# Nine modulation vectors per layer: three move one FFN stage later, and three of the first stage change from VectorE alone to VectorE, GpSimd and ScalarE

## The chip, the core and the metric

The kernel runs on one core of a Trainium2 chip. The core has a matrix engine (TensorE, PE in the rows), an elementwise engine (VectorE, DVE), an activation engine (ScalarE, ACT), a programmable engine (GpSimd, POOL) and an engine that here only issues transfers (SyncE, SP). Each works through its own instructions in order. The metric is device time in microseconds (us), the median of the runs; less is better.

## What is computed

Two layers of a diffusion backbone over 256 latent and 256 context tokens of width 1024. Each layer is FFN, token mixer, FFN; every one of these has a shift, a scale and a gate, which are slices of one modulation product per layer and stream. Cut to what matters here:

```python
act_l = jax.nn.silu(c)
act_c = jax.nn.silu(c_ctx)
for i in range(DEPTH):
    mod_l = (act_l @ w_mod[i] + b_mod[i])[:, None, :]          # 9 vectors of 1024
    mod_c = (act_c @ w_mod[i][:, :n_c] + b_mod[i][:n_c])       # 9 in layer 0, 5 in layer 1
    ...
def ffn_sublayer(x, mods, base, g_pre, g_post, w_in, w_out):
    h = modulated_norm(x, g_pre, mods[base], mods[base + 1])
    return x + 0.5 * mods[base + 2] * rms_norm(swiglu(h, w_in, w_out), g_post)
```

Vectors 0 to 2 belong to the first FFN of a layer, 3 to 5 to its mixer, 6 to 8 to its second FFN.

## The kernel before

**Matrix work.** Every weight is brought as chunks of 128x1024 f32. SyncE loads a chunk into a ring of four buffers ("raw"); ScalarE rounds it into `wh` (L220), VectorE makes the rest `wl` = raw - wh (L221), and TensorE does three products for each pair (L227, L228, L229; 24 matmuls of 512 columns for a chunk, called a unit below). `wh` and `wl` have three buffers each. TensorE's order is written out by hand and is the same in both kernels; the other engines' orders come from a scheduler that follows the program's emission order and a few marks (`after`).

**The modulation vectors.** One vector is eight tiles of 128x1024 of `w_mod`. A tile is multiplied by the activation (a broadcast row `act`) and summed along its row, once for the context stream and once for the latent stream (layer 1's vectors 5 to 8 need the latent stream alone). `mod_flow` knows two ways for a tile with two streams:

- "both on VectorE" (`both`, layer 0 with j >= JB): two VectorE instructions `jk` (L329), each with its sum.
- "split": one `jk` on VectorE for the latent stream, then GpSimd multiplies the tile in place by the context row (L333), then ScalarE sums it (L306). The tile's buffer is free only after that sum.

A tile with one stream is one `jk`.

**Where the tiles go.** They are spread over the units of three FFN stages; `stepper` is called once a unit and hands out tiles at a rate (a sum of costs over a total) after a number of skipped units. Stage A is the first FFN of layer 0 (about 60 to 460 us): its tiles share the raw ring with the weights and are loaded by SyncE, and beside them GpSimd computes the set-up of a state space (S5) (L205 to L210 on tiles `s5...`), whose tables SyncE writes out with eight transfers (`s5d<-s5tab`); a hyena filter is computed too. Stage B is the second FFN of layer 0 (about 1212 to 1560 us), stage C the first FFN of layer 1 (about 1595 to 1945 us). In B and C a tile has a ring of its own with two buffers (`mraw`), and its load is issued by GpSimd (L298), in order between GpSimd's other work. B and C also make the S5 tables of layer 1 (`s5_tables`, one slice per eight units in B and per five in C), which go back and forth between GpSimd (`bb`, `vvt`, L1191 to L1213), VectorE (`rin`, `wt`, L205 to L210, L1222 to L1224), ScalarE (`rin`), TensorE (`pn`, L1230, L1240) and transfers.

Per unit of its second part, a stage thus has on VectorE: `wl`, the gate (L547, L548, and `gg`, L234, per two units), the `jk`s, and in B and C the table work.

Of the kernel before, what the change touches and what calls it, by code (L numbers as in the profile page):

```python
# [79 lines left out]
RAW0 = 16  # L80
WPF = 2
OW = 1.0
JB = 5


def layout(i):
# [77 lines left out]
def build(tc, A):  # L164
# [10 lines left out]
    def dma(o, i):  # L175
        return nc.sync.dma_start(o, i)

    def after(*ins):

        stack = ExitStack()  # L180
        for i in ins:
            stack.enter_context(tc.issue_after(i.ins))
        return stack

    with st, tc.manual_schedule(engines={mybir.EngineType.PE}):
# [71 lines left out]
        def mod_steps(l, js, act, raw=None):  # L257
            if callable(act):
                act = act()
            for j in js:  # L260
                ss = [1] if l == 1 and j >= 5 else [0, 1]
                for k in range(KT):
                    w = raw() if raw else rp.tile([P, D], F32, tag="raw", name="raw")
                    dma(w, A["wmod"][l, j, k])
                    c = j * KT + k
                    both = l == 0 and j >= JB
                    for s in ss if both else [1]:
# [17 lines left out]
        def mod_flow(l, js, act, raw=None):  # L285

            if callable(act):
                act = act()  # L290
            tiles = [(j, k) for j in js for k in range(KT)]
            ws, back = {}, []

            def load(n):
                if n < len(tiles):
                    j, k = tiles[n]
                    ws[n] = raw() if raw else rp.tile([P, D], F32, tag="raw", name="raw")
                    (G.dma_start if raw else dma)(ws[n], A["wmod"][l, j, k])  # L298

            def finish():  # L300
                while back:
                    back.pop(0)()

            def sums(w, s, c):
                with after(mark["wh"]):
                    S.activation(w, w, AF.Copy, scale=0.5, accum_out=md[l][:, s, c : c + 1])  # L306

            def bias(j, ss):
                for s in ss:
                    m = md[l][:, s, j * KT : (j + 1) * KT]  # L310
                    V.tensor_tensor(m, m, bmt[l][:, j * KT : (j + 1) * KT], op=ALU.add)

            if raw:
                load(0)
                yield
            for n, (j, k) in enumerate(tiles):
                finish()
                if not raw:
                    load(n)
                c = j * KT + k  # L320
                w = ws.pop(n)
                ss = [1] if l == 1 and j >= 5 else [0, 1]
                both = l == 0 and j >= JB
                fast = ss if both else [1]
                slow = [s for s in ss if s not in fast]
                for s in fast:
                    jk = sp.tile([P, D], BF16, tag="sq", name="jk", bufs=1)
                    with after(mark["wl"]):
                        V.scalar_tensor_tensor(  # L329
                            jk, w, 0.5, act[s], op0=ALU.mult, op1=ALU.mult, accum_out=md[l][:, s, c : c + 1]  # L330
                        )
                for s in slow:
                    G.tensor_tensor(w, w, act[s], op=ALU.mult)  # L333
                    back.append(lambda w=w, s=s, c=c: sums(w, s, c))
                if k == KT - 1:
                    back.append(lambda j=j, ss=ss: bias(j, ss))
                if raw:
                    load(n + 1)
                yield
            finish()  # L340
# [6 lines left out]
        def pre_coeff(l, base, gi, streams):  # L347
            a = cp.tile([P, 2, KT], F32, tag="pa", name="pa", bufs=2)
            for s in streams:
                V.scalar_tensor_tensor(  # L350
                    a[:, s], md[l][:, s, (base + 1) * KT : (base + 2) * KT], 1.0, ngt[l][:, gi], op0=ALU.add, op1=ALU.mult
                )
                V.tensor_scalar(a[:, s], a[:, s], RMS_D, None, op0=ALU.mult)
            return lambda s, k: (a[:, s, k : k + 1], md[l][:, s, base * KT + k : base * KT + k + 1])

        def gate_rows(l, base, gi, fac, streams):
            gr = cp.tile([P, 2, D], F32, tag="grow", name="grow", bufs=1)
            gc = cp.tile([P, 2, KT], F32, tag="gc", name="gc", bufs=2)
            for s in streams:
                V.scalar_tensor_tensor(  # L360
                    gc[:, s], md[l][:, s, (base + 2) * KT : (base + 3) * KT], fac * RMS_D, ngt[l][:, gi], op0=ALU.mult, op1=ALU.mult
                )
            s0, n = streams[0], len(streams)
            ps = psy.tile([P, 512], F32, tag="py", name="psg")
            T.transpose(ps[: n * KT, :P], gc[:, s0:].rearrange("p s k -> p (s k)"), ident)
            gs = sp.tile([P, 512], F32, tag="t", name="gs")[:, :P]
            S.activation(gs[: n * KT], ps[: n * KT, :P], AF.Copy)
            gd = dp.tile([1, 2 * D], F32, tag="gd", name="gd", bufs=2)
            dma(gd[:, : n * D].rearrange("o (k p) -> (o k) p", p=P), gs[: n * KT])
            dma(gr[:, s0:].rearrange("p s d -> p (s d)"), gd[:, : n * D].to_broadcast([P, n * D]))  # L370
            return gr
# [229 lines left out]
        def act_load():  # L601
            a = [xp.tile([P, D], F32, tag="xr", name="act") for _ in range(2)]
            for s in range(2):
                dma(a[s], actd[s].to_broadcast([P, D]))
            return a
# [29 lines left out]
        def stepper(gens, total, skip=0):  # L635

            todo = [g for g, _ in gens]
            rate = sum(c for _, c in gens) / total
            state = {"credit": 0.0, "skip": skip}

            def step(weight):
                if state["skip"]:
                    state["skip"] -= 1
                    return
                state["credit"] += rate * weight
                while todo and state["credit"] > 1e-6:
                    try:
                        next(todo[0])
                        state["credit"] -= 1.0
                    except StopIteration:  # L650
                        todo.pop(0)

            return step
# [15 lines left out]
        with ExitStack() as fs:  # L669
# [127 lines left out]
                        acts.extend(act_load())  # L797
                return acts

            st0 = stepper([(mod_flow(0, [2, 3, 4], acts0), 25), (mod_flow(0, [5, 6, 7, 8], acts0), 33)], 46, 12)  # L800

            half = [0]

# [11 lines left out]
        for l in range(L):  # L815
            last = l == L - 1
            toks = TLAT if last else TALL
            streams = [1] if last else [0, 1]

            nx = dict(src=xd, out=None, keep=toks)  # L820
            late = mixer(E, l, h, late, toks, streams, nx)
            h = nx["h"]

            with ExitStack() as fs:
                gp = Gates(fs, f"B{l}")
                if last:
                    n3 = dict(src=xd, out=A["out"], keep=[])
                    ffn(l, 1, h, late, toks, n3, gp, lambda w: None, lambda: gate_rows(l, 6, 5, 0.5, streams), lambda: None)
                else:
                    n3 = dict(src=xd, out=None, keep=TALL)  # L830

                    def fill1():
                        n3.update(coeff=pre_coeff(1, 0, 0, [0, 1]), h=new_h())

                    x1, raw1 = mod_ring(fs, "mrB")
                    st1 = stepper([(mod_flow(1, [0, 1, 2, 3, 4], act_load, raw1), 42)], 50, 4)
                    tg1 = ahead(fs, gp, "s5p", range(0, 3))

                    def step1(w):
                        st1(w)  # L840
                        tg1()

                    late = ffn(l, 1, h, late, toks, n3, gp, step1, lambda: gate_rows(l, 6, 5, 0.5, streams), fill1, xpool2=x1)
                    h = n3["h"]
            if not last:
                with ExitStack() as fs:
                    gp = Gates(fs, "C")
                    n4 = dict(src=xd, out=None, keep=TLAT)

                    def fill2():  # L850
                        n4.update(coeff=pre_coeff(1, 3, 2, [0, 1]), h=new_h())

                    x2, raw2 = mod_ring(fs, "mrC")
                    st2 = stepper([(mod_flow(1, [5, 6, 7, 8], act_load, raw2), 34)], 50, 4)
                    tg2 = ahead(fs, gp, "s5q", range(3, 8))

                    def step2(w):
                        st2(w)
                        tg2()

                    late = ffn(1, 0, h, late, TALL, n4, gp, step2, lambda: gate_rows(1, 0, 1, 0.5, [0, 1]), fill2, xpool2=x2)
                    h = n4["h"]
# [1395 lines left out]
```

## Time and profile before

| what | value |
|---|---|
| median of 3 runs | 2597.41 us (2596.99 to 2599.07) |
| the profiled execution | 2597.24 us |
| its span in the trace | 2595.4 us |
| TensorE busy | 2482.5 us, 96% |
| VectorE busy | 1750.1 us, 67% |
| ScalarE busy | 1079.3 us, 42% |
| GpSimd busy | 671.6 us, 26% |

The span is the time from the first to the last instruction of the profiled execution. Busy shares are means over stages that differ much: VectorE has 67% over the span, and far more in parts of A, B and C.

### The profile page before, as it was taken

What the parts mean: (1) busy time and instruction counts of PE and PEld (TensorE: products, weight loads), DVE (VectorE), ACT (ScalarE), POOL (GpSimd) and SP (SyncE); (2) the same over time, 40 slices, a digit from 0 to 9 for tenths busy, and PEclk for the clock granted to TensorE, in tenths of its full rate; (3) what the DMA queues carried; (4) which work ended last, traced back from release to release, by engine and by line L of the source; (5) the groups of instructions that cost most, each with busy time, mean ns of one, the idle gap of its engine ahead of it and who ended that gap; (6) DMA issues with size and microseconds to landing.
All of it is one profiled execution on the core that took longest, in us unless ns stands there. A gap on an engine that the chain in (4) does not pass through costs nothing. (4 is left out here: it accounts for less than half of the span.)

```text
span 2595.4 us, 38077 instructions
## 1 busy us (share of the span) xinstructions
PE 2482.5 (96%) x14606; PEld 2096.0 (81%) x14606; DVE 1750.1 (67%) x2624; ACT 1079.3 (42%) x1828; POOL 671.6 (26%) x692
## 2 busy tenths in 40 slices
PE   6988999999999898999999999999999999998998
PEld 3866888887778776888778888888889889997996
DVE  6888995455645798557998637885435667776664
ACT  5345323454543223434444424332234555355443
POOL 4894000100101784003665403540001012000000
PEclk8999999999999999999999999999999999999999
DMA  6336675223232232343565544676542335865564
GB/s 244 107 118 229 233 256 194 78 82 82 75 109 86 76 97 86 105 159 135 190 213 203 196 162 148 223 239 189 173 138 78 94 111 179 324 227 197 179 192 133
DMA packets 138819, 411.07 MB, mean 158 GB/s; under 512 B 27096, under 2 KB 45321, under 8 KB 135821
## 3 DMA queue, kind: packets, MB, share of 16 engines
q1 hardware_dynamic: 124812, 353.61, 41.8%
q0 software_dynamic: 12672, 45.59, 5.2%
q10 hardware_dynamic: 1152, 9.44, 0.9%
q8 instruction: 115, 1.88, 0.3%
q14 instruction: 68, 0.55, 0.1%
HBM read 374.41 MB, written 34.16 MB: 157 GB/s over the span
## 5 line engine op out<-in xcount | busy, mean ns | idle before, releaser
L221 DVE TENSOR_TENSOR wl<-raw,wh 128x1024 fp32r<-128x1024 f32 x424 | 557.1, 1314 | 468.2 <-ACT wh L220 461.4
L220 ACT ACTIVATE wh<-raw 128x1024 fp32r<-128x1024 f32 x424 | 448.9, 1059 | 748.0 <-issue 184.8
L229 PE MATMUL pin<-hh,wl 128*128 128x512 f32 (+1 forms) x1468 | 529.9, 361 | 18.7 <-DVE wl L221 18.6
L227 PE MATMUL pin<-hh,wh 128*128 128x512 f32 (+1 forms) x1468 | 531.6, 362 | 11.8 <-DVE hh L415 7.8
L228 PE MATMUL pin<-hl,wh 128*128 128x512 f32 (+1 forms) x1468 | 528.7, 360 | 1.7 <-DVE hl L418 1.6
L229 PEld LDWEIGHTS pin<-hh,wl 128*128 128x128 f32 x1468 | 282.5, 192 | 64.7 <-DVE wl L221 24.9
L227 PEld LDWEIGHTS pin<-hh,wh 128*128 128x128 f32 x1468 | 282.8, 193 | 56.9 <-DVE hh L415 9.4
L228 PEld LDWEIGHTS pin<-hl,wh 128*128 128x128 f32 x1468 | 282.6, 193 | 42.7 <-DVE hl L418 3.1
L246 POOL TENSOR_TENSOR r<-v,mhalf 128x1 f32<-128x1 f32 (+2 forms) x46 | 31.4, 682 | 1030.4 <-DVE v L245 931.8
L1345 PE MATMUL pm<-hh,wh 128*128 128x512 f32 (+1 forms) x704 | 251.5, 357 | 0.0
L1347 PE MATMUL pm<-hh,wl 128*128 128x512 f32 (+1 forms) x704 | 245.2, 348 | 0.2 <-DVE wl L221 0.2
L1346 PE MATMUL pm<-hl,wh 128*128 128x512 f32 (+1 forms) x704 | 245.0, 348 | 0.0
L461 PE MATMUL y<-wh,gg 128*128 128x512 f32 x448 | 177.2, 396 | 0.0
L463 PE MATMUL y<-wh,gg 128*128 128x512 f32 x448 | 177.2, 396 | 0.0
L462 PE MATMUL y<-wl,gg 128*128 128x512 f32 x448 | 177.2, 396 | 0.0
L1345 PEld LDWEIGHTS pm<-hh,wh 128*128 128x128 f32 x704 | 134.1, 190 | 18.1 <-issue 2.5
L1347 PEld LDWEIGHTS pm<-hh,wl 128*128 128x128 f32 x704 | 133.8, 190 | 17.8 <-DVE wl L221 0.4
L1346 PEld LDWEIGHTS pm<-hl,wh 128*128 128x128 f32 x704 | 134.1, 191 | 15.0
L329 DVE SCALAR_TENSOR_TENSOR jk<-raw,act 128x1024 bf16<-128x1024 f32 x88 | 117.6, 1336 | 5.0 <-DMA raw<-wmod 4.1
L333 POOL TENSOR_TENSOR mraw<-mraw,act 128x1024 f32<-128x1024 f32 x40 | 102.6, 2565 | 49.6 <-DVE jk L329 48.3
L227 PE MATMUL pm<-hh,wh 128*128 128x256 f32 (+1 forms) x320 | 103.5, 324 | 0.0
L228 PE MATMUL pm<-hl,wh 128*128 128x256 f32 (+1 forms) x320 | 102.7, 321 | 0.1
(481 smaller groups left out, 4933.0 us busy)
## 6 DMA issues: line engine op xcount, KB each, us to landing
raw<-fin SPq DMA_DIRECT2D x176, 512.0 KB, 3.6
raw<-winf SPq DMA_DIRECT2D x122, 512.0 KB, 3.6
mraw<-wmod POOLq DMA_DIRECT2D x72, 512.0 KB, 4.8
raw<-wmod SPq DMA_DIRECT2D x64, 512.0 KB, 4.4
raw<-foa SPq DMA_DIRECT2D x64, 512.0 KB, 3.5
raw<-wbr SPq DMA_DIRECT2D x32, 512.0 KB, 3.6
raw<-fob SPq DMA_DIRECT2D x24, 512.0 KB, 4.1
s5tabd<-rin ACTq DMA_DIRECT2D x8, 1152.0 KB, 7.4
```

Source lines behind the costliest of these rows:

```text
L220: mark["wh"] = S.activation(wh, w, AF.Copy)
L221: mark["wl"] = V.tensor_tensor(wl, w, wh.bitcast(F32), op=ALU.subtract)
L227: T.matmul(out, lhsT=lh, rhs=rh, start=first and i == 0, stop=False)
L228: T.matmul(out, lhsT=lh, rhs=rl, start=False, stop=False)
L229: T.matmul(out, lhsT=ll, rhs=rh, start=False, stop=last and i == n - 1)
L329: V.scalar_tensor_tensor(jk, w, 0.5, act[s], op0=ALU.mult, op1=ALU.mult, accum_out=md[l][:, s, c : c + 1])
L461: T.matmul(o, lhsT=lh, rhs=rh, start=kt == 0, stop=False)
L462: T.matmul(o, lhsT=lh, rhs=rl, start=False, stop=False)
L463: T.matmul(o, lhsT=ll, rhs=rh, start=False, stop=kt == nk - 1)
L1345: T.matmul(o, lhsT=lh, rhs=rh, start=i == 0, stop=False)
L1346: T.matmul(o, lhsT=lh, rhs=rl, start=False, stop=False)
L1347: T.matmul(o, lhsT=ll, rhs=rh, start=False, stop=i == n - 1)
```

## The change

`JB` goes from 5 to 8, so that vectors 5, 6 and 7 of layer 0 are split as 2, 3 and 4 are. Vector 8 of layer 0 moves from A to B (still both on VectorE, at the head of B, with B's private ring), and vectors 3 and 4 of layer 1 move from B to C (still split, at the head of C). The rates and skips follow.

```diff
-JB = 5
+JB = 8
...
-            st0 = stepper([(mod_flow(0, [2, 3, 4], acts0), 25), (mod_flow(0, [5, 6, 7, 8], acts0), 33)], 46, 12)
+            st0 = stepper([(mod_flow(0, [2, 3, 4, 5, 6, 7], acts0), 49)], 50, 10)
...
                     x1, raw1 = mod_ring(fs, "mrB")
-                    st1 = stepper([(mod_flow(1, [0, 1, 2, 3, 4], act_load, raw1), 42)], 50, 4)
+                    acts1 = []
+
+                    def act1():
+                        acts1.extend([] if acts1 else act_load())
+                        return acts1
+
+                    st1 = stepper([(mod_flow(0, [8], act1, raw1), 10), (mod_flow(1, [0, 1, 2], act1, raw1), 26)], 48, 4)
...
                     x2, raw2 = mod_ring(fs, "mrC")
-                    st2 = stepper([(mod_flow(1, [5, 6, 7, 8], act_load, raw2), 34)], 50, 4)
+                    st2 = stepper([(mod_flow(1, [3, 4, 5, 6, 7, 8], act_load, raw2), 50)], 54, 4)
```

Counted over the program:

| stage | tiles a unit, before | after | `jk` (L329) | L333 and L306 | tile loads |
|---|---|---|---|---|---|
| A | 58/46 = 1.26, from unit 13 | 49/50 = 0.98, from unit 11 | 88 to 48 | 24 to 48 | 56 to 48, SyncE |
| B | 42/50 = 0.84 | 36/48 = 0.75 | 40 to 40 | 40 to 24 | 40 to 32, GpSimd |
| C | 34/50 = 0.68 | 50/54 = 0.93 | 32 to 48 | 0 to 16 | 32 to 48, GpSimd |

**SyncE in A, round the eight S5 dumps.** The rows are SyncE's transfers in order; `raw<-fin` loads a weight chunk, `raw<-wmod` a tile, `raw<-hw` and `Hd<-H` belong to the hyena filter. Before:

```order
L176 DMA raw<-hw 64x1024
L176 DMA raw<-fin 128x1024
L176 DMA raw<-wmod 128x1024
L176 DMA raw<-fin 128x1024
L176 DMA raw<-wmod 128x1024
L176 DMA Hd_110<-H 128x512 x2
L176 DMA s5d_108<-s5tab 128x552 x4
L176 DMA s5d_109<-s5tab 128x552 x4
L176 DMA raw<-fin 128x1024
```

And now:

```order
L176 DMA raw<-hw 64x1024
L176 DMA raw<-fin 128x1024
L176 DMA raw<-wmod 128x1024
L176 DMA raw<-fin 128x1024
L176 DMA Hd_110<-H 128x512
L176 DMA raw<-wmod 128x1024
L176 DMA raw<-fin 128x1024
L176 DMA Hd_110<-H 128x512
L176 DMA s5d_108<-s5tab 128x552 x4
L176 DMA s5d_109<-s5tab 128x552 x4
L176 DMA raw<-wmod 128x1024
```

Between the hyena load and the dumps stand now three weight chunks instead of two: the 23rd chunk of the program is issued ahead of the dumps and no longer behind them.

**GpSimd in C, one slice of the tables.** `bb` and `vvt` are the slice's tables, `mraw<-wmod` a tile's load, L333 the multiplication of a tile. Before, from the load ahead of the slice:

```order
L1194 TENSOR_SCALAR prm<-prm 128x64
L298 DMA mraw<-wmod 128x1024 x2
L206 TENSOR_TENSOR tmp<-prm,s5t 128x4x16
L1191 MEMSET bb 128x16
L205 TENSOR_TENSOR bb<-prm,s5t 128x64
L208 TENSOR_TENSOR bb<-prm,s5t 128x64
L1197 TENSOR_TENSOR vvt<-s5t,prm 128x576
L1210 TENSOR_TENSOR vvt<-s5t,prm 128x576
L207 TENSOR_TENSOR bb<-bb,tmp 128x64
```

The same piece now (line numbers from 840 on are larger by 6):

```order
L333 TENSOR_TENSOR mraw<-mraw,act 128x1024
L206 TENSOR_TENSOR tmp<-prm,s5t 128x4x16
L298 DMA mraw<-wmod 128x1024
L333 TENSOR_TENSOR mraw<-mraw,act 128x1024
L1197 MEMSET bb 128x16
L205 TENSOR_TENSOR bb<-prm,s5t 128x64
L208 TENSOR_TENSOR bb<-prm,s5t 128x64
L1203 TENSOR_TENSOR vvt<-s5t,prm 128x576
L1216 TENSOR_TENSOR vvt<-s5t,prm 128x576
L298 DMA mraw<-wmod 128x1024
L207 TENSOR_TENSOR bb<-bb,tmp 128x64
```

Tile loads and tile multiplications stand now in the middle of the slice, a load even between the parts of `bb`. A load there waits until ScalarE has summed the tile that had its buffer.

## Rows read from the trace of the kernel before

**Rows 1.** The page: busy us (share) xinstructions; a group: busy, mean ns, idle before.
```profile
PE 2482.5 (96%) x14606; PEld 2096.0 (81%) x14606; DVE 1750.1 (67%) x2624; ACT 1079.3 (42%) x1828; POOL 671.6 (26%) x692
...
L220 ACT ACTIVATE wh<-raw 128x1024 fp32r<-128x1024 f32 x424 | 448.9, 1059 | 748.0 <-issue 184.8
```

**Rows 2.** Stretches: length, busy us (instructions) of each engine, clock, DMA.
```profile
218.00:263.00 45.00, 41.55 (x172) 32.37 (x170) 42.42 (x50) 25.38 (x37) 24.44 (x9) 0.96 0.53 184
263.00:330.00 67.00, 67.00 (x296) 55.20 (x295) 64.89 (x104) 24.67 (x35) 3.21 (x2) 1.00 0.68 229
...
1222.00:1345.00 123.00, 118.35 (x572) 96.05 (x571) 116.78 (x124) 51.98 (x84) 82.26 (x69) 0.99 0.58 191
...
1600.00:1742.00 142.00, 142.00 (x774) 118.30 (x773) 120.14 (x167) 49.48 (x76) 63.96 (x91) 1.00 0.68 223
```

**Rows 3.** TensorE's waits, 100 to 700 us: total, times, longest.
```profile
PE pin L229 <- DVE wl L221: 14.0, 8, 4.0
```

**Rows 4.** TensorE's waits, 1260 to 1400 us.
```profile
PE pin L229 <- DVE wl L221: 4.7, 5, 2.1
```

**Rows 5.** GpSimd's instructions, 190 to 204 us: start, duration.
```profile
194.86 1.20 POOL L210 TENSOR_TENSOR s5ni<-s5ni,s5pt 128x64 f32<-128x64 f32 x1
```

**Rows 6.** SyncE's transfers, 190 to 210 us: issue, duration.
```profile
197.28 6.95 SPq L176 DMA_DIRECT2D s5d<-s5tab  x8
204.42 0.56 SPq L176 DMA_DIRECT2D raw<-fin  x1
```

**Rows 7.** TensorE, 205 to 216 us.
```profile
212.52 0.50 PE L227 MATMUL pin<-hh,wh 128*128 128x512 f32 x1 [3.98 <-ACT wh L220]
```

**Rows 8.** VectorE, 1279 to 1287 us.
```profile
1280.03 0.68 DVE L548 SCALAR_TENSOR_TENSOR t<-t,pin 128x512 f32<-128x512 f32 x1
1280.62 2.85 DVE L221 TENSOR_TENSOR wl<-raw,wh 128x1024 fp32r<-128x1024 f32 x1
```

**Rows 9.** GpSimd, 1279 to 1287 us.
```profile
1280.00 2.39 POOL L333 TENSOR_TENSOR mraw<-mraw,act 128x1024 f32<-128x1024 f32 x1 [3.56 <-DVE jk L329]
```

**Rows 10.** VectorE's groups in B, 1222 to 1344 us.
```profile
L221 DVE TENSOR_TENSOR wl<-raw,wh 128x1024 fp32r<-128x1024 f32 x20 | 33.6, 1680 | 1.1 <-ACT wh L220 1.1
...
L234 DVE TENSOR_TENSOR gg<-t,gg 128x512 fp32r<-128x512 f32 x11 | 16.3, 1481 | 0.0
L1224 DVE TENSOR_TENSOR wt<-wt,t 128x512 f32<-128x512 f32 x6 | 9.6, 1593 | 0.2
```

**Rows 11.** GpSimd's groups in B, 1222 to 1344 us.
```profile
L333 POOL TENSOR_TENSOR mraw<-mraw,act 128x1024 f32<-128x1024 f32 x16 | 41.4, 2589 | 29.0 <-DVE jk L329 28.1 <-DVE md L311 0.8
L298 POOL DMA_DIRECT2D mraw<-wmod x15 | 9.0, 598 | 10.4 <-ACT mraw L306 10.4
```

**Rows 12.** VectorE's groups in C, 1606 to 1742 us.
```profile
L329 DVE SCALAR_TENSOR_TENSOR jk<-mraw,act 128x1024 bf16<-128x1024 f32 x16 | 20.6, 1290 | 0.0
...
L234 DVE TENSOR_TENSOR gg<-t,gg 128x512 fp32r<-128x512 f32 x12 | 8.4, 699 | 0.0
...
L1222 DVE TENSOR_TENSOR wt<-s5t,bb 128x512 f32<-128x512 f32 x8 | 7.7, 962 | 5.7 <-POOL bb L207 5.7
...
L1224 DVE TENSOR_TENSOR wt<-wt,t 128x512 f32<-128x512 f32 x10 | 6.8, 683 | 0.1
...
L205 DVE TENSOR_TENSOR rin<-s5t 128x256 f32<-128x256 f32 x4 | 2.7, 687 | 8.1 <-DMA s5tabd<-rin 8.1
L206 DVE TENSOR_TENSOR t<-s5t 128x256 f32<-128x256 f32 x4 | 2.0, 494 | 3.1 <-DMA s5t<-s5d 3.1
```

**Rows 13.** VectorE in C, 1604 to 1612 us.
```profile
1606.82 1.23 DVE L221 TENSOR_TENSOR wl<-raw,wh 128x1024 fp32r<-128x1024 f32 x1 [0.47 <-ACT wh L220]
```

**Rows 14.** GpSimd in C, 1660 to 1668 us.
```profile
1664.76 2.29 POOL L1212 TENSOR_TENSOR vvt<-vvt,tmp 128x576 f32<-128x576 f32 x1
```

**Rows 15.** TensorE in C, 1678 to 1684 us.
```profile
1680.58 1.03 PE L1230 MATMUL pn<-ident,wt 128*128 128x128 f32 x8
1681.54 1.08 PE L1240 MATMUL pn<-vvt,bb 64*32 64x128 f32 x32
```

## What the change will do to the time

> **What bounds the kernel now.** I read the page first: TensorE is busy 2482.5 us, 96% of the 2595.4 us span [rows 1], so only 113 us can be won, and a change off TensorE counts only where it makes TensorE wait. The question for each stage is therefore whether `wl`, the last step of a weight chunk, comes in time. In a stretch without waits TensorE does 296 matmuls in 67 us [rows 2], that is 4.42 per us, and a unit of 24 matmuls takes 5.43 us. I use that rate to turn counts into lost time.
>
> A, up to 263 us, loses time. Its `wl` comes late eight times, 14.0 us in all [rows 3]. The longest single wait, 3.98 us, ends at 212.52 and is on `wh` [rows 7]. What lies behind it: the S5 chain on GpSimd ends at 194.86 + 1.20 [rows 5], SyncE then issues the eight dumps from 197.28 on, 6.95 us, and the next weight chunk stands behind them and is issued at 204.42 [rows 6]. From 218 to 263 us TensorE does 172 matmuls where 45 us hold 199: 27 fewer, 6.1 us, with VectorE busy 42.42 of 45 [rows 2]. From 263 us on nothing is lost.
>
> B loses 4.7 us in waits on `wl` between 1260 and 1400 us [rows 4]. By counts: 572 matmuls, of which 80 are table work in two rounds and 492 make 20.5 units; 111.3 us and two rounds of 2.0 us (1680.58 to 1681.54 + 1.08 [rows 15]) are 115.4 of the 123 us [rows 2]. So about 7.6 us go, with VectorE busy 116.78 of 123.
>
> C loses nothing before: TensorE is busy 142.00 of 142 us, VectorE 120.14 and GpSimd 63.96 [rows 2]. It is no idle stage, though, and the change puts work into it.
>
> **What a split tile costs VectorE.** While L333 ran from 1280.00 to 1282.39 [rows 9], a `wl` that began at 1280.62 took 2.85 us [rows 8], against 1.23 for one alone [rows 13]; the L548 that reads PSUM took 0.68 beside the same L333 [rows 8]. So VectorE's instructions with two SBUF operands stand still while GpSimd multiplies. The cost in the mean: beside the 16 L333 of B [rows 11], 20 `wl` took 1680 ns, 11 `gg` 1481, 6 L1224 1593 [rows 10]; undisturbed they take 1230 [rows 13], 699 and 683 [rows 12]. That is 9.0 + 8.6 + 5.5 = 23 us, 1.5 us per L333 (part of it is the table work's doing; other instructions that waited are not counted). The upper bound is the whole L333, 2.39 us. A split tile so costs VectorE 1.29 [rows 12] + 1.5 to 2.4 = 2.8 to 3.7 us, and a tile with both streams on VectorE 2.6. Splitting relieves VectorE of nothing; only fewer tiles per unit do.
>
> The Trainium skill says the same of the sharing ("GPSIMD Engine Reference", section "Key points"): GpSimd shares its SBUF interfaces with VectorE and contends with VectorE instructions in a two-port mode or with two SBUF inputs, and VectorE is about twice as fast on elementwise work. By that rule splitting is the wrong direction, and each L333 costs VectorE up to its whole length; the rows agree for a single instruction and give less in the mean. With it C would cost 32 instead of 25 below.
>
> **The change, stage by stage.**
>
> *A, the dumps.* One more weight chunk stands ahead of the dumps on SyncE, and the GpSimd chain that they wait for is no shorter: the same eleven L333 lie ahead of its end. TensorE so has one more unit to do while the dumps are issued: -5.4 us, one unit, which takes up the 3.98 us wait. If that chunk comes late itself: 0.
>
> *A, 218 to 263 us.* 0.98 tiles per unit in place of 1.26: 0.28 tiles less, at 2.8 us each 0.8 us of VectorE per unit, 6.3 us over the eight units. That covers the 6.1 lost: -5.5, between 0 and -6.1.
>
> *A after 263 us.* VectorE had 1.26 x 2.6 = 3.3 us of tiles per unit and now has 0.98 x 2.8 = 2.7. No loss before, none expected: 0. But a split tile keeps its buffer of the shared ring for the L333 and the sum longer; if that makes chunks 0.3 us late in each of some 30 units, +9.
>
> *B.* Its first ten to eleven units now carry 8 tiles with two `jk` and no L333, then 0.75 split tiles a unit. Over its 20 chunks that is some 7 `jk` more (+9 us of VectorE) and 9 L333 fewer (-14 to -22). Of the 7.6 us lost, 5 to all come back: -6, between -3 and -7.6. GpSimd, with nine L333 less, makes the tables earlier.
>
> *C.* The 16 split tiles come at 0.93 per unit, so within 17 units. These take TensorE 17 x 5.43 + 3 rounds of tables x 2.0 = 98.3 us. VectorE's demand: of its 120.14 in 142 us, 83.2 fall on 98.3 us; 16 `jk` in place of 12 add 5.2; 16 L333 add 24 at 1.5 and 38 at 2.39; its waits for the table chain, 5.7 + 8.1 + 3.1 = 16.9 us in 136 [rows 12], are 12.2. These waits do not vanish when VectorE gets busier, since it waits in order. Together 124.6 to 138.6 us. Against that stand 98.3 us and the lead at the start: with three buffers for `wh` a chunk is copied when TensorE ends the unit three back, so the lead is two units, 10.9, less 1.06 for the copy [rows 1] and 1.23 for `wl` [rows 13]: 8.6 us. TensorE loses 17.7 to 31.7 us.
>
> GpSimd decides where in that span. Its 63.96 us in 142 are 44.3 in 98.3; 16 L333 at 2.59 add 41.4, four loads 2.4, and waits of a load for the sum before it 16 x 10.4/15 = 11.1 [rows 11]: 99.2 of 98.3 us, so it is full. In B before it was not (82.26 of 123, [rows 2]). Before, no tile of C is split and its loads wait for a `jk` at most. Now a load that waits for a sum stands between the two halves of `bb`, which VectorE's L1222 needs; what queues behind L1222 on VectorE is the next `wl`. The margin of the tables (L1212 ends at 1664.76 + 2.29 [rows 14], TensorE needs them at 1680.58 [rows 15]: 13.5 us) goes too, and then TensorE waits for the tables as well. I take +25, the middle; stepping the four queues row by row through the new order with these durations comes to 27 for this piece, and to none for the order of before. If the table waits melt and only the L333 count: 12.2 less, +5.5.
>
> After its first 17 units C is as before, with one `jk` a tile; the sums on ScalarE (16 x 1.15) lie in its idle time.
>
> *Sum.* -5.4 - 5.5 + 0 - 6 + 25 = +8.1. The profiled execution took 2597.24 us, 0.17 under the median of the runs shown; 2605.3 us.
>
> **The rivals.** A difference under 0.2%, 5.2 us, counts as none.
> - *C pays only for part of it.* The waits for tables shrink where VectorE gets to them later, and C loses 13 to 19: 2593 to 2599, no change. For it: VectorE has 21.9 us idle in 142, and a busy engine comes later to a table that is then there. Against it: the tables come later as well. Chance 0.27.
> - *C absorbs it (faster).* The shut-outs fall on VectorE's idle time, and the GpSimd chain keeps its margin of 13.5 us: C loses 0 to 11, at 5.5 2585.8 us. It decides as soon as C costs less than 12. For it: in A VectorE is 64.89 of 67 us busy and TensorE loses nothing [rows 2]. Against it: A has no table chain there. Chance 0.15.
> - *The whole L333 shuts VectorE out.* C costs 32 and B gives back all 7.6: 2610.7 us. If A's split tiles also hold the ring, another 9: 2620. Chance 0.13. This is the rule of the Trainium skill named above.
> - *The unit ahead of the dumps is not won,* since the first L333 come earlier on GpSimd and push the chain: 5.4 more, 2610.7. Chance 0.05 by itself, counted with the last.
>
> **How the numbers follow.** The forecast, C at 20 to 30, has 0.40: 2600 to 2610. With 0.27 for the first rival, 0.15 for the second and 0.18 for the last two the range that leaves out no more than two in ten runs from 2590, inside the second rival, to 2615, inside the third. Faster by over 0.2% (under 2592.2) is the second rival and the low end of the first: 0.17. Slower (over 2602.6) is the last two and three quarters of the forecast, 0.48, and a little of the first's spread: 0.50. Same: 0.33.
>
> **What would show it.** In the profile after: TensorE in C no longer 142 of 142, with waits on `wl` and on the tables (`pn`) between about 1600 and 1720 us, and `wl`, `gg` and L1224 longer there; GpSimd over 90% busy or waiting for sums. In B the waits on `wl` gone or under 2 us. In A the 3.98 us wait gone, and 218 to 263 us near 199 matmuls. The prediction is wrong if C shows under 12 us of waits, or if A after 263 us waits at all.

## The result and the profile after

The changed kernel takes 2624.36 us (median of 4 runs, 2619.08 to 2629.71) against 2598.24 (4 runs) before: a ratio of 1.0100, 95% interval 1.0082 to 1.0118. It is slower, as forecast, but by 26 us and not 8, and lies above the range. The profiled execution has a span of 2622.3 us, 26.9 more than before.

TensorE runs the same instructions in the same order, so each has a shift: its start after less its start before. What a stage costs is the difference of the shifts at its ends.

| stage, and the instruction read at its end | before | after | shift | cost | predicted |
|---|---|---|---|---|---|
| A up to the dumps (`psm`, L943 after) | 225.9 | 226.2 | +0.3 | +0.3 | -5.4 |
| A from there (`psm`, L965) | 266.4 | 260.6 | -5.8 | -6.1 | -5.5 |
| A, the rest (first `pt` behind it) | 459.4 | 455.7 | -3.6 | +2.2 | 0 |
| mixer of layer 0, last `psg` | 1148.0 | 1145.3 | -2.8 | +0.8 | 0 |
| B, first `pt` behind it | 1567.6 | 1557.2 | -10.4 | -7.6 | -6 |
| C, last round of tables (`pn`) | 1744.6 | 1770.7 | +26.1 | +36.5 | +25 |
| the rest | | | +26.9 | +0.8 | 0 |

(Shifts come from unrounded starts.) B and the second part of A came about as worked out; C cost 11.5 us more than forecast, and the dumps in A did not give their 5.4.

From the page of the changed kernel, the busy row, which answers to [rows 1], and the two groups of the tiles' multiplications on GpSimd:

```profile
PE 2483.9 (95%) x14606; PEld 2096.5 (80%) x14606; DVE 1751.4 (67%) x2576; ACT 1105.3 (42%) x1876; POOL 738.2 (28%) x724
...
L333 POOL TENSOR_TENSOR raw<-raw,act 128x1024 f32<-128x1024 f32 x48 | 123.9, 2582 | 122.6 <-DVE jk L329 104.7
...
L333 POOL TENSOR_TENSOR mraw<-mraw,act 128x1024 f32<-128x1024 f32 x40 | 103.2, 2580 | 57.4 <-DVE jk L329 56.2
```

VectorE has 48 instructions less and is 1.3 us busier: splitting took nothing off it. TensorE does the same work; it waits longer and, behind its waits, runs slower.

TensorE's waits after, in order: three rows of A (60 to 500 us), the longest of B (1210 to 1590), and all of C (1590 to 1990):

```profile
PE pin L229 <- DVE wl L221: 10.2, 5, 4.5
PE psm L965 <- DVE c L957: 6.3, 1, 6.3
PE pin L227 <- ACT wh L220: 5.7, 1, 5.7
...
PE pt L396 <- DVE xn L386: 3.1, 1, 3.1
...
PE pin L229 <- DVE wl L221: 17.1, 7, 5.5
PE pn L1236 <- DVE wt L1230: 6.2, 2, 3.2
PE pn L1246 <- POOL vvt L1218: 1.0, 1, 1.0
```

In A the waits on `wl` shrank ([rows 3]: 14.0), but the one on `wh` is 5.7 instead of 3.98 [rows 7], and a wait of the hyena filter's product (`psm`) is new. It costs nothing in the end: TensorE is 8.1 us late behind it (144.0 us) and 2.5 early at 189.3, since the kernel before has waits of its own there (3.97 us on `wl`, among those of [rows 3], and 3.85 us of `psm` on the hyena filter's `H`, which ends at 190.78 us). In B no wait on `wl` is left [rows 4]. In C, which had none [rows 2], 24.3 us stand: on `wl` and on the tables, as predicted. The rest of C's 36.5 us is for the most part matmuls that ran at a lower clock behind these waits (last section).

The stretches of [rows 2] after, and the twenty chunks of C from the third `wl` to the 23rd, with the same columns:

```profile
218.00:263.00 45.00, 44.58 (x185) 35.63 (x186) 43.65 (x50) 26.01 (x38) 20.82 (x8) 0.95 0.55 187
263.00:330.00 67.00, 65.98 (x287) 53.08 (x286) 56.38 (x65) 33.18 (x53) 26.35 (x11) 1.00 0.57 190
...
1222.00:1345.00 123.00, 123.00 (x637) 101.65 (x636) 107.09 (x140) 47.14 (x74) 57.67 (x60) 1.00 0.61 195
...
1597.61:1757.28 159.67, 136.56 (x686) 108.78 (x684) 140.75 (x157) 59.14 (x99) 110.86 (x107) 0.95 0.57 193
```

The same twenty chunks before, a row not shown so far:

```profile
1606.82:1729.49 122.67, 122.67 (x666) 101.34 (x665) 102.43 (x140) 41.12 (x67) 62.33 (x88) 1.00 0.70 227
```

VectorE needs 37.0 us more for these chunks: it is busy 38.3 us more (102.43 to 140.75) and idle 1.3 us less (20.24 to 18.92). What filled its time after, as groups of VectorE in that stretch, and what it waited for there:

```profile
L221 DVE TENSOR_TENSOR wl<-raw,wh 128x1024 fp32r<-128x1024 f32 x21 | 37.2, 1769 | 0.5 <-ACT wh L220 0.5
L329 DVE SCALAR_TENSOR_TENSOR jk<-mraw,act 128x1024 bf16<-128x1024 f32 x19 | 28.9, 1522 | 17.1 <-DMA mraw<-wmod 17.1
L234 DVE TENSOR_TENSOR gg<-t,gg 128x512 fp32r<-128x512 f32 x11 | 12.9, 1170 | 0.0
...
L1230 DVE TENSOR_TENSOR wt<-wt,t 128x512 f32<-128x512 f32 x8 | 9.2, 1154 | 0.0
```

```profile
DVE jk L329 <- DMA mraw<-wmod: 17.1, 4, 7.7
DVE wt L1228 <- POOL bb L207: 1.3, 1, 1.3
DVE wl L221 <- ACT wh L220: 0.5, 1, 0.5
```

Two things are to be seen. `gg` takes 1170 ns and L1230 1154, where [rows 12] have 699 and 683 (L1224 is L1230 now). Five `jk` more, 19 for 14, are 6.5 us at 1.30; the other 31.8 us are nearly all instructions that stand still, some 2.0 us for each of the 16 L333. And the waits have changed their cause: of the 16.9 us for tables [rows 12] 1.3 are left, but 17.1 us of waits for the tile itself (`jk` for `mraw`) have come.

A piece of the timeline after, three engines in C. Columns: start, duration, instruction, idle before it:

```profile
1695.01 2.39 POOL L333 TENSOR_TENSOR mraw<-mraw,act 128x1024 f32<-128x1024 f32 x1 [3.48 <-DVE jk L329]
1695.44 3.04 DVE L221 TENSOR_TENSOR wl<-raw,wh 128x1024 fp32r<-128x1024 f32 x1
...
1725.30 1.06 ACT L306 ACTIVATE mraw<-mraw 128x1024 f32<-128x1024 f32 x1 [3.64 <-POOL mraw L333]
...
1729.38 2.37 POOL L333 TENSOR_TENSOR mraw<-mraw,act 128x1024 f32<-128x1024 f32 x1 [1.77 <-DVE jk L329]
1731.71 1.44 POOL L1200 TENSOR_SCALAR prm<-prm 128x64 f32<-128x64 f32 x1
...
1733.99 1.13 POOL L298 DMA_DIRECT2D mraw<-wmod  x2
...
1745.13 1.23 DVE L329 SCALAR_TENSOR_TENSOR jk<-mraw,act 128x1024 bf16<-128x1024 f32 x1 [7.71 <-DMA mraw<-wmod]
```

The first pair is a shut-out: a `wl` of 3.04 us beside an L333, as in [rows 8, 9]. The rest is the longest wait for a tile: ScalarE has summed one tile by 1726.4, so its buffer is free, but the load into it stands on GpSimd behind the next L333 and table work until 1733.99, is issued together with the one for the other buffer, and VectorE's next `jk` begins at 1745.13.

### The profile page after: what moved, and what is told of

Same layout as the page of the kernel before. It is cut to its first block, busy times and chain, and to the rows that moved or that the text cites. A ratio compares the mean times of both kernels' runs of the same rounds, so it can differ in the third digit from the quotient of the medians.

```text
span 2622.3 us, 38111 instructions
## 1 busy us (share of the span) xinstructions
PE 2483.9 (95%) x14606; PEld 2096.5 (80%) x14606; DVE 1751.4 (67%) x2576; ACT 1105.3 (42%) x1876; POOL 738.2 (28%) x724
## 5 line engine op out<-in xcount | busy, mean ns | idle before, releaser
L221 DVE TENSOR_TENSOR wl<-raw,wh 128x1024 fp32r<-128x1024 f32 x424 | 578.8, 1365 | 474.3 <-ACT wh L220 466.4
L229 PE MATMUL pin<-hh,wl 128*128 128x512 f32 (+1 forms) x1468 | 528.5, 360 | 27.4 <-DVE wl L221 27.3
L229 PEld LDWEIGHTS pin<-hh,wl 128*128 128x128 f32 x1468 | 281.5, 192 | 73.2 <-DVE wl L221 33.6
L333 POOL TENSOR_TENSOR raw<-raw,act 128x1024 f32<-128x1024 f32 x48 | 123.9, 2582 | 122.6 <-DVE jk L329 104.7
L1353 PEld LDWEIGHTS pm<-hh,wl 128*128 128x128 f32 x704 | 133.4, 190 | 17.8 <-DVE wl L221 0.4
L329 DVE SCALAR_TENSOR_TENSOR jk<-mraw,act 128x1024 bf16<-128x1024 f32 x88 | 114.1, 1297 | 20.4 <-DMA mraw<-wmod 20.4
L333 POOL TENSOR_TENSOR mraw<-mraw,act 128x1024 f32<-128x1024 f32 x40 | 103.2, 2580 | 57.4 <-DVE jk L329 56.2
L298 POOL DMA_DIRECT2D mraw<-wmod x80 | 45.2, 565 | 225.3 <-DVE jk L329 160.1
```

The costliest lines, as they stand in the source:

```text
L221: mark["wl"] = V.tensor_tensor(wl, w, wh.bitcast(F32), op=ALU.subtract)
L229: T.matmul(out, lhsT=ll, rhs=rh, start=False, stop=last and i == n - 1)
L1353: T.matmul(o, lhsT=ll, rhs=rh, start=False, stop=i == n - 1)
```

## The experiments

Two theories of C were to be told apart: that the time goes because **tiles come late** (loads stand in GpSimd's queue), and that **VectorE's own time** is what counts (the instructions that L333 stops). For A: whether splitting or the earlier start (unit 11, not 13) takes the gain. Edits are against the changed kernel, unless said otherwise. Ratios are against runs of the kernel before that were made beside each run; their medians lay between 2598.32 and 2601.06 us. Costs of stages are by shifts of the profiled executions, against the kernel before; C counts from the first `pt` behind B to the stage's end.

**C with vectors 3 and 4 both on VectorE**, no L333 there:

```diff
-                both = l == 0 and j >= JB
+                both = l == 0 and j >= JB or l == 1 and j in (3, 4)
```

> The changed kernel with one thing different: in stage C vectors 3 and 4 of layer 1 are multiplied for both streams on VectorE (32 jk for 16 tiles, no L333, no L306, rate kept). Two theories of the 35.3 us that C lost. Late tiles: a tile's load stands in GpSimd's queue behind tables, L333 and sums, the tile lands late (17.1 us of VectorE's idle time end with a tile's landing), and the next wl queues behind its jk; then this kernel, whose tiles are free after their jk, loses in C only what VectorE's own demand asks: 83.2 us plus 20 jk of 1.29 is 109 against 98.3 and 8.6 of lead, +2, with the table waits at most +14, so 2591 to 2603 us. VectorE's time: any two-stream tile costs VectorE 2.6 us or more, and C stays expensive whoever multiplies, +18 to +30, 2607 to 2619 us.

Measured: 2605.33 us, ratio 1.0019 (1.0010 to 1.0028); C costs 18.5 us. Its waits of TensorE in C and, between 1590 and 1770 us, none of VectorE on a tile:

```profile
PE pn L1236 <- DVE wt L1230: 11.5, 4, 4.4
PE pin L229 <- DVE wl L221: 1.4, 1, 1.4
```

Two `jk` a tile cost half of what one `jk` and an L333 cost. The time lies between what the two theories gave, so this one does not decide.

**The loads of these tiles from ScalarE's queue**, all else as changed:

```diff
-                    (G.dma_start if raw else dma)(ws[n], A["wmod"][l, j, k])
+                    (S.dma_start if l == 1 and j in (3, 4) else G.dma_start if raw else dma)(ws[n], A["wmod"][l, j, k])
```

> The changed kernel with one thing different: in stage C the 16 loads of vectors 3 and 4 are issued by ScalarE, right behind the sum that frees the buffer, and no longer by GpSimd; L333 and sums stay. Late tiles: the loads come some us earlier, the 17.1 us that VectorE idles for tiles fall to under 6 and the time by 8 to 20, to 2604 to 2616 us. VectorE's time (16 L333 that shut VectorE out for 1.5 to 2.4 us each): nothing changes, 2620 to 2628 us.

Measured: 2610.72 us, ratio 1.0045 (1.0028 to 1.0061); C costs 23.6 us, 12.9 less than with GpSimd's loads. VectorE's two longest waits, 1590 to 1770 us:

```profile
DVE jk L329 <- DMA mraw<-wmod: 3.2, 3, 2.3
DVE wl L221 <- ACT wh L220: 2.1, 3, 1.4
```

So with the loads out of GpSimd's queue the tiles are hardly late, and 12.9 of C's 36.5 us are gone. The rest stays although VectorE is hardly idle any more.

**C without the 16 multiplications on GpSimd:**

```diff
-                    G.tensor_tensor(w, w, act[s], op=ALU.mult)
+                    if l == 0 or j < 3:
+                        G.tensor_tensor(w, w, act[s], op=ALU.mult)
```

> The changed kernel without the 16 L333 of stage C (the context stream of vectors 3 and 4 is then the plain sum of the tile; loads on GpSimd and sums on ScalarE stay). VectorE's time: the shut-outs go with them, 24 to 38 us, and C costs no more than 5, 2590 to 2596 us. Late tiles: GpSimd's queue is 41 us shorter, but the loads still wait for sums and tables in order; C keeps 8 to 15 us, 2598 to 2606 us.

Measured: 2588.84 us, ratio 0.9955 (0.9940 to 0.9970); C costs 1.4 us, and TensorE has no wait in it. The stretch 1610 to 1770 us, columns as in [rows 2]:

```profile
1610.00:1770.00 160.00, 160.00 (x861) 131.92 (x860) 139.47 (x191) 68.63 (x112) 78.49 (x102) 1.00 0.77 254
```

35 of the 36.5 us go with the L333, the late tiles' share among them (6.5 us of VectorE's waits for tiles are left, and they cost TensorE nothing). Sixteen tiles more, their `jk`, loads and sums on ScalarE, are not what C cannot bear.

**Vectors 5 and 6 ahead of 3 and 4 in C:**

```diff
-                    st2 = stepper([(mod_flow(1, [3, 4, 5, 6, 7, 8], act_load, raw2), 50)], 54, 4)
+                    st2 = stepper([(mod_flow(1, [5, 6, 3, 4, 7, 8], act_load, raw2), 50)], 54, 4)
```

> The changed kernel with one thing different: in stage C the order of the vectors is 5, 6, 3, 4, 7, 8, so that the 16 split tiles come in units 21 to 39 instead of 4 to 21; the five rounds of S5 tables end by unit 30. Both theories have the price come from the L333 beside the tables; with about half of the tiles behind the last round C costs 12 to 20 in place of 35, 2603 to 2611 us. If the price hangs on the split tiles alone, wherever they stand, it stays at 2620 to 2628 us.

Measured: 2596.43 us, ratio 0.9983 (0.9973 to 0.9993); C costs 7.8 us, less than expected. Eight of the 16 L333 now start after 1765 us, past the last table slice on GpSimd, and TensorE's waits on `wl` in C are 3.8 us. The same 16 split tiles in the same stage so cost 29 us less in another place.

**A: the kernel before, with vectors 5 to 8 split in place and none moved:**

```diff
-JB = 5
+JB = 9
...
-            st0 = stepper([(mod_flow(0, [2, 3, 4], acts0), 25), (mod_flow(0, [5, 6, 7, 8], acts0), 33)], 46, 12)
+            st0 = stepper([(mod_flow(0, [2, 3, 4, 5, 6, 7, 8], acts0), 58)], 46, 12)
```

> The kernel before with one thing different: vectors 5 to 8 of layer 0 in stage A are split too (56 split tiles at the old rate of 1.26 a unit; B and C as before). It separates the splitting in A from its lower rate. Splitting relieves VectorE of nothing (a split tile costs it 1.3 and the shut-out of 1.5 to 2.4, a tile with two jk 2.6): A gets no faster, and with each tile holding its buffer of the shared ring through L333 and the sum it loses 3 to 20 us after 263 us, 2603 to 2620 against 2600 for the kernel before. Rival, that the split itself is what helped A: 2590 to 2597.

Measured: 2613.28 us, ratio 1.0059 (1.0047 to 1.0072). The shift is +1.6 us at 266 us and +16.1 at the end of A. TensorE's waits, 60 to 500 us:

```profile
PE pin L229 <- DVE wl L221: 23.1, 14, 3.8
PE pin L227 <- ACT wh L220: 5.6, 3, 3.9
PE y L462 <- DVE wl L221: 2.6, 4, 0.9
```

A split tile in the place of one with two `jk` is a loss by itself, and 14.5 of the 16.1 us come after 266 us, where the kernel before loses nothing [rows 2]. So what A gains in the changed kernel is not the splitting; the last run of this section has the fewer tiles alone.

**A with the start of before, after 12 units:**

```diff
-            st0 = stepper([(mod_flow(0, [2, 3, 4, 5, 6, 7], acts0), 49)], 50, 10)
+            st0 = stepper([(mod_flow(0, [2, 3, 4, 5, 6, 7], acts0), 49)], 48, 12)
```

> The changed kernel with the first tile of A two units later (skip 12 and a total of 48, 1.02 tiles a unit). The changed kernel has a new wait of 6.3 us at 130 us, on the hyena filter, behind copies that wait for an S5 chain on GpSimd that has an L333 in front. If the end of that chain at 196 us bounds this stretch, the wait is hidden: A stays within 2 us of the changed kernel's, 2621 to 2627 us. If the wait lies on the path, 5 to 6 us come back: 2616 to 2620 us.

Measured: 2620.74 us, ratio 1.0083 (1.0069 to 1.0097). The hyena wait is gone and the one on `wh` is 2.3 us. The shift is -4.2 us at the 225.9 us of before, -10.3 at 266.4 and -8.0 at A's end: the 4.4 us more than in the changed kernel all come by the dumps in this pair of profiles. SyncE issues them here from 189.83 us on:

```profile
189.83 5.52 SPq L176 DMA_DIRECT2D s5d<-s5tab  x8
```

Profiles of one order differ, though. The eight kernels whose A is that of the changed kernel show -0.9 to +0.3 us by the dumps and -3.6 to -5.8 at A's end; the two with these tiles and the start after 12 units, this one and the first under "The best of it", -4.2 and -2.4, and -8.0 and -8.2. So the earlier start takes 2.2 to 4.6 us from A, of which 1.5 to 4.5 show by the dumps. The whole time does not tell it by itself, as its interval overlaps that of the changed kernel.

**Both edits of C together** (vectors 5 and 6 first, 3 and 4 both on VectorE):

> The changed kernel with two things different in C: order 5, 6, 3, 4, 7, 8, and vectors 3 and 4 on VectorE alone (no L333 in C). With the split tiles late C cost 7.7 us, with two jk early 18.5. If the L333 beside the tables are what is left, C costs 0 to 4 and the time is 2585 to 2592; if VectorE's own 20 jk are too many wherever they stand, C costs 8 or more, 2596 or above.

Measured: 2592.60 us, ratio 0.9973 (0.9963 to 0.9983), C at 2.7 us. **The same with 7 ahead of 3 and 4 as well**, and a quicker rate:

```diff
-                    st2 = stepper([(mod_flow(1, [3, 4, 5, 6, 7, 8], act_load, raw2), 50)], 54, 4)
+                    st2 = stepper([(mod_flow(1, [5, 6, 7, 3, 4, 8], act_load, raw2), 50)], 46, 2)
```

> As the last, with the order 5, 6, 7, 3, 4, 8 and 1.09 tiles a unit from the third unit on, so that vectors 3 and 4 stand in units 24 to 39, for the greater part behind the tables, and the one-stream tiles come faster beside the tables. If only work beside the tables costs, C costs 0 to 3, 2585 to 2590 us, unless the higher rate of one-stream tiles (0.16 more of 1.3 us a unit than before) fills VectorE beside the tables: then 4 to 8 us more.

Measured: 2594.41 us, ratio 0.9982 (0.9973 to 0.9991), C at 7.9 us: the 0 to 3 of the expectation failed, and its second case (4 to 8 us more, from the higher rate) came. Order and rate were changed together, so that it is the rate is not shown.

**Vectors 3 and 4 of layer 1 back in B**, A as changed, C as before:

```diff
-                    st1 = stepper([(mod_flow(0, [8], act1, raw1), 10), (mod_flow(1, [0, 1, 2], act1, raw1), 26)], 48, 4)
+                    st1 = stepper([(mod_flow(0, [8], act1, raw1), 10), (mod_flow(1, [0, 1, 2, 3, 4], act1, raw1), 42)], 51, 4)
...
-                    st2 = stepper([(mod_flow(1, [3, 4, 5, 6, 7, 8], act_load, raw2), 50)], 54, 4)
+                    st2 = stepper([(mod_flow(1, [5, 6, 7, 8], act_load, raw2), 34)], 50, 4)
```

> One part of the change undone: vectors 3 and 4 of layer 1 go back to B (B then has vector 8 of layer 0 and vectors 0 to 4 of layer 1, 48 tiles at 1.02 a unit), C is as before; A as changed. If L333 and loads beside tables cost as in C, B pays it with its sparser tables: 10 to 25 us more than the kernel before in B, 2603 to 2620 us. If a split tile costs only where tables come every five units, B costs under 5 and the time is 2592 to 2600.

Measured: 2615.91 us, ratio 1.0064 (1.0049 to 1.0080). B costs 17.8 us, C 0.9. What VectorE, and then TensorE, waited for in B (1210 to 1590 us), two rows each:

```profile
DVE wl L221 <- ACT wh L220: 50.7, 19, 4.4
DVE jk L329 <- DMA mraw<-wmod: 29.1, 24, 2.4
...
PE pin L229 <- DVE wl L221: 9.7, 6, 3.5
PE y L462 <- DVE wl L221: 4.5, 2, 2.9
```

So C's loss belongs to the moved vectors alone, and moving them is worth 25.4 us to B (17.8 less -7.6), which vector 8 then takes up in part.

**The best of it:** C's two edits with A's start after 12 units:

> What the runs so far point to, together: the changed kernel with A's first tile two units later (skip 12, total 48), and in C the order 5, 6, 3, 4, 7, 8 with vectors 3 and 4 on VectorE alone. If the stages add up (A -8, B -6, C +3 against the kernel before): 2586 to 2591 us. If A's two units later only moved noise, A gives -5 and the time is 2590 to 2594.

Measured: 2588.09 us, ratio 0.9960 (0.9948 to 0.9973). **And vectors 5 to 7 of layer 0 both on VectorE as well:**

```diff
-                both = l == 0 and j >= JB
+                both = l == 0 and j >= 5 or l == 1 and j in (3, 4)
```

> As the last, and vectors 5 to 7 of layer 0 in A are on VectorE alone again, at the lower rate (JB for A is 5, vector 8 stays in B). If splitting is a cost in A as well (16 us at the old rate), A gains another 1 to 4 us, 2583 to 2589. If at the lower rate A has room for it after 263 us, the two are the same within 2 us.

Measured: 2586.09 us, ratio 0.9953 (0.9939 to 0.9967), faster than the kernel before and the changed one; its interval overlaps that of the run above, so the last edit is not shown to help. C costs 1.1 us with all its 48 tiles. A is here the kernel before with vector 8 taken out and the lower rate, nothing split anew and the same start: TensorE's shift at A's end is -9.5 us. So fewer tiles a unit alone give A at least what the changed kernel has there (-3.6). Its stretch there:

```profile
1610.00:1770.00 160.00, 159.65 (x825) 131.04 (x824) 146.38 (x209) 51.78 (x79) 70.11 (x97) 1.00 0.73 246
```

VectorE is busy 146.38 of 160 us and TensorE waits 0.4.

## Why the prediction was wrong

The sign, the place of the loss and its kind were right. Two terms of the sum were not: C's credit, and the unit won by the dumps.

**C, +25, measured +36.5.** The step that failed is the credit more than the demand. For the twenty chunks the demand is 38.3 us of VectorE's busy time: 6.5 of `jk` and 31.8 of shut-outs, 2.0 us each, in the middle of the 1.5 to 2.39 that the prediction set (its middle is 36.2 us more). Against it the prediction put, for its 17 units, a lead of 8.6 us and 2.9 us of slack (98.3 - 83.2 - 12.2). Of the lead too little was there: the 23rd `wl` of before ends at 1730.72 and TensorE needs it at 1734.17, so 3.45 us were left of it beside the tables. Of VectorE's idle time 1.3 us were used. 38.3 - 1.3 - 3.45 is 33.6, and TensorE's shift over these chunks goes from -9.2 to +24.4, just that. Of the 11.5 us that the forecast missed, some 6.8 are this credit (11.5 put, 4.75 there) and 2.1 the demand; 2.9 lie outside the twenty chunks, where the prediction had nothing: 1.1 ahead of them and 1.7 behind the last wait (last section). Nor was GpSimd full, as the prediction had it (99.2 of 98.3 us): it is busy 110.86 of 159.67 us, its loads wait 5.7 us for sums where 11.1 were put, and its L333 wait 14.6 us for VectorE's `jk` (without the wait that began ahead of the stretch). The buffers of `wh` gave the most that the lead can be; the row of the `wl` beside the tables would have given what it was.

**The waits that "do not vanish".** The prediction kept 12.2 us of VectorE's idle time since it waits in order. The time stayed (20.2 and 18.9 us), but for another reason than the one given: the table waits nearly went, as the first rival had it, and waits for tiles came in their place, from the loads between GpSimd's table work, which the prediction named as a load on `bb` and not on the tile's own `jk`. Loads from ScalarE, with both kinds of wait nearly gone, still cost 23.6, far over the 5.5 that the prediction gave for that case (13.3 with the 31.8 us measured for the L333): the lead and the slack it counted on were not there.

**The third rival** came closest with 2620, by a sum that was not right either: C at 32 was near, but A's nine lost microseconds after 263 us were 2.2, of which TensorE's waits show 1.0 (TensorE 65.98 of 67 us busy in the row above, 67.00 in [rows 2]); that it came near is in part luck. By the prediction's own sign, that A should not wait at all there, it was wrong here too, by this 1.0 us. The split in place shows that the fear was no idle one: at 1.26 tiles a unit A loses 14.5 us there (by the ring, as this rival has it, or by VectorE, busy 165.81 of the 194 us from 266 to 460 and 152.17 before: not parted). The Trainium skill's rule ("GPSIMD Engine Reference", section "Key points"), that GpSimd contends with VectorE's instructions with two SBUF inputs, agrees with 3.04 us for a `wl` beside an L333, where one alone took 1.23 [rows 13]. Taken as the whole L333 each time it would be 40.8 us (16 x 2.55, from its rows in C) where 31.8 were measured.

**The dumps, -5.4, measured +0.3.** Here the last rival came out, which had 0.05 by itself. The step that failed is the credit of a whole unit: it took it that the dumps, bound by the GpSimd chain, go out as before, and that what stands behind them does not matter. The chain was indeed no later. Its last write of a table, VectorE's copy of it and SyncE's wait, first before (SyncE's longest, 180 to 215 us), then after:

```profile
191.95 0.75 POOL L210 TENSOR_TENSOR s5pw<-s5pw,s5pt 128x256 f32<-128x256 f32 x1
...
SPq L176 <- DVE w3l L929: 9.5, 1, 9.5
```

```profile
191.91 0.75 POOL L210 TENSOR_TENSOR s5pw<-s5pw,s5pt 128x256 f32<-128x256 f32 x1
...
195.80 2.42 DVE L1100 COPY s5tab<-s5pw 128x128 f32<-128x128 f32 x1
...
SPq L176 <- DVE s5tab L1101: 2.8, 1, 2.8
```

The prediction misread [rows 5]: that instruction's result is used nowhere, and the kernel before does not wait for the tables at all. Their last copy ends at 196.55 us, and the dumps follow in SyncE's order behind `Hd` at 197.28; what held SyncE ahead of that was a hyena weight (`w3l`). After, SyncE does wait for the tables, 2.8 us: the last copies stand on VectorE behind a `jk`, and one of them takes 2.42 us while the L333 of 195.75 runs. The earlier start does push the chain, as the rival says: started after 12 units, its last write ends at 182.76 and not at 192.66.

The timeline of A after: first an L333 in the S5 chain at 116 us and what it does to VectorE and TensorE, then GpSimd, VectorE, SyncE, ScalarE and TensorE round the dumps:

```profile
116.02 2.39 POOL L333 TENSOR_TENSOR raw<-raw,act 128x1024 f32<-128x1024 f32 x1
...
121.12 0.20 DVE L1112 COPY s5s_c<-s5nr 128x64 f32<-128x64 f32 x1 [5.61 <-POOL s5nr L207]
...
130.61 0.79 PE L965 MATMUL psm<-w,c 128*128 128x512 f32 x1 [6.29 <-DVE c L957]
...
198.14 0.40 DVE L1101 COPY s5tab<-s5pw 128x128 f32<-128x128 f32 x1
...
198.57 5.05 SPq L176 DMA_DIRECT2D s5d<-s5tab  x8
203.72 0.57 SPq L176 DMA_DIRECT2D raw<-wmod  x1
...
209.56 1.23 DVE L329 SCALAR_TENSOR_TENSOR jk<-raw,act 128x1024 bf16<-128x1024 f32 x1 [4.96 <-DMA raw<-wmod]
...
216.97 0.42 ACT L952 ACTIVATE cur<-a 64x256 f32<-64x256 f32 x1 [6.43 <-DVE a L950]
217.29 1.04 ACT L220 ACTIVATE wh<-raw 128x1024 fp32r<-128x1024 f32 x1
218.38 0.80 PE L227 MATMUL pin<-hh,wh 128*128 128x512 f32 x1 [5.72 <-ACT wh L220]
```

The last copy of the tables ends at 198.54 and the dumps start at 198.57, 1.3 us later than before [rows 6] and 8.7 later than with the start after 12 units. The further chunk is ahead of them, and TensorE is 2.5 us early at 189.3. But then comes what the prediction did not follow, the queues behind SyncE's: a tile is loaded behind the dumps, VectorE waits 4.96 us for it, the hyena step `a` stands behind that `jk`, ScalarE waits 6.43 for `a`, and `wh` stands behind on ScalarE. That a tile loaded ahead of the dumps would take this wait away was not tried.

**A from 218 to 263 us, -5.5, measured -6.1:** right, with no wait on `wl` there any more. The stretch holds 185 matmuls and not near 199, the sign that the prediction named, because the 5.72 us wait ends in it, with a lower clock behind (last section).

**B, -6, measured -7.6**, all that the stretch had lost [rows 2]; VectorE's busy time fell from 116.78 to 107.09 us.

## What to carry to other kernels

Beside a VectorE that is busy with instructions of two SBUF inputs, a multiplication moved to GpSimd was no relief: here it took 2.0 us from VectorE, more than the 1.3 us that it replaced, and its place beside a busy VectorE decided nearly all of the loss (36.5 us at the stage's head, 7.8 two vectors later, 2.7 there as a second `jk`). When a lead is credited, read it off the row where the late instruction of before ended and was used, not from the number of buffers. A load that is issued from an engine's queue comes as late as that engine's work; so follow a moved step through every in-order queue behind it, also those of the engines that it only feeds.

## What was not expected of the hardware

TensorE's granted clock fell where it waited: 0.95 in the twenty chunks of C, 1.00 before. The first matmul behind the 5.51 us wait that ends at 1709.78 takes 0.79 us, and 0.80 behind the 5.72 us one in A, where others take 0.39: the lower of the two levels, 1.2 GHz for 2.4. Mean matmuls of L229 in C (1590 to 1770 us) grew from 389 to 406 ns. Two stretches behind waits, with the columns of [rows 2]:

```profile
1709.78:1714.00 4.22, 4.22 (x10) 3.35 (x11) 4.22 (x7) 0.00 (x0) 1.77 (x1) 0.50 0.75 258
...
1758.60:1763.00 4.40, 4.40 (x12) 3.48 (x13) 4.37 (x9) 0.60 (x2) 1.02 (x2) 0.61 0.87 289
```

Over the twenty chunks TensorE's shift grows by 25.1 us at nine waits of over 1 us and by 8.5 in between, about what a granted clock of 0.95 over 159.67 us takes (8.0). VectorE, the bound there, shows no wait for TensorE, so a quicker clock would most likely have waited longer for the next `wl`; no run parts the two. Behind the last wait nothing takes the lower clock up any more: from 1758.60 to 1763.00 us the shift grows from 24.4 to 26.1, so this 1.7 us is a cost of its own.

The tile loads that GpSimd issued between 1717 and 1747 us took 3.6 to 11.7 us to land, in the middle 7.9, against 4.7 over the whole program; a split tile gives its buffer back late, so that two loads are issued together. How much of C's late tiles is this and how much the queue stays open: the run with ScalarE's loads changed both.
